# One 512-column matmul for the z projection, its halves added at eviction, and modulation sums moved to the first out-projection

## The chip, the core and the metric

One NeuronCore of a Trainium2 chip runs the whole program. The metric is the device time of one execution in microseconds (us), lower is better. Engines are named as in the profile: PE (TensorE, matmuls; PEld its weight loads), DVE (VectorE), ACT (ScalarE), POOL (GpSimd), SP (SyncE, whose queue issues nearly all DMAs).

## The reference

Two layers on x of shape (1, 256, 2048), all float32. A conditioning vector gives each layer shift, scale and gate by a product with `ada_w`. Layer 0 is chunked gated linear attention, layer 1 an S5 state-space mixer. What the change touches is layer 0:

```python
mod = einsum('bd,lde->lbe', silu(c), ada_w) + ada_b
u = x * (1 + scale) + shift
proj = u @ w_in                                   # 2048 x 10256
q, k, v, z, g_lr = split(proj, ...)               # z: 4096 columns
...
o = o * rsqrt(mean(square(o)) + eps)              # per head of 1024 channels
y = (o * norm_g) * silu(z)
h = y @ w_out                                     # 4096 x 2048, the first out-projection
x = layer_norm(alpha * x + (1 + gate) * h, ...)
```

## The kernel before, in words

Every large product is made of three: each float32 operand is split into a high part (ACT casts it to fp32r, line 145) and the rest (DVE subtracts, line 146), and high x high, high x low and low x high are summed in PSUM. A weight tile is 256 rows by 512 columns (512 KB); a step loads one (`wload`, line 136), splits it into `hi` and `lo` (rings of three buffers each), and multiplies. `st_step` (lines 171 to 182) keeps the weights stationary and streams u's 256 tokens: for each of 4 column blocks and 2 row blocks three matmuls of 256 columns, high weights by u high (L180), high weights by u low (L181), low weights by u high (L182). `st_wide` (lines 184 to 193) is used so far by the GLU product (`gl`) alone: u's two parts lie side by side (`Pairs`), so that the high weights meet both in one matmul of 512 columns (L192) and the low weights meet u high in one of 256 (L193); the two halves of the bank are added when it is read (L1323, L1324).

The stages of layer 0: q, k and v in four blocks of rows; then z in 8 groups of 512 columns with 8 steps each (lines 884 to 900); then the first out-projection, `op` (`out_proj`, line 902), 4 column groups of 16 steps. Step (g, kp) below is step kp of group g of z, or of column group g of op. Beside the z steps, the heads of the attention are finished piece by piece (`head`, line 842): in an even group one piece a step, two PE products `pso` and three evictions (`og`, `sq` or `sqt`); then once a head the root of a mean (`psrms`, ACT's Sqrt into `sd`, L865), DVE's reciprocal (L868) and two multiplications of `og` (L872), and after the odd group `og` by silu(z) (`head_fin`, L880). At the end of each z group ACT reads the four banks with Silu (L896) into time-permuted order. There are five banks in that PSUM pool. `pump(rate)` spreads background steps over the main steps: mostly the modulation's sums (`ada_dve`, line 290), where one step loads 512 KB of `ada_w` and makes two DVE multiply-adds (L309, `acc`), and every ninth finishes a block of 512 columns. `Z_RATE` and `OP_RATE` (line 663) are background steps per main step; what is left in `bg` passes from stage to stage. A scheduler may then exchange neighbouring instructions of an engine; each engine runs its list in order.

Of the kernel before, what the change touches and what calls it, by code (L numbers as in the profile page):

```python
# [8 lines left out]
F32 = mybir.dt.float32  # L9
F32R = mybir.dt.float32r  # L10
# [23 lines left out]
def trunk(ctx, tc, x, c, ln_g, ln_b, ada_w, ada_b, gla_w_in, gla_gate_w2, gla_gate_b, gla_norm_g,  # L34
# [39 lines left out]
    def s8t(name, shape, dt=F32):  # L74
        return s8.tile([P] + shape, dt, tag="s8", name=name)
# [265 lines left out]

    u0 = Parts([s8t(f"u0h{i}", [8, T], F32R) for i in range(2)], [s8t(f"u0l{i}", [8, T], F32R) for i in range(2)])

# [316 lines left out]
    for part in range(2):  # L660
        for j in range(4):
            bg.extend(ada_dve(1, part, j))
    V_RATE, Z_RATE, OP_RATE = 0.825, 0.944, 0.755
    KEEP = (4, 6)
# [172 lines left out]


    zt_ = [s8t(f"z{h}", [8, T]) for h in range(4)]
    og, sq = [None] * 4, [None] * 4  # L840

    def head(h):
        def o_step(vt_):
# [6 lines left out]
            PE.matmul(ps[:, 128:256], lhsT=vtok[:, 1, f * P:(f + 1) * P], rhs=sts[:, h, 256:384], start=False, stop=True)  # L850
            S.activation(og[h][:, vt_, :], ps[:, :T], AF.Identity, scale=gnT[:, f:f + 1])
            if vt_ == 0:
# [8 lines left out]
        def rms():  # L861
            ps = psx(f"psrms{h}")
            PE.matmul(ps[:, :T], lhsT=ones, rhs=sq[h], start=True, stop=True)
            sd[0] = tp.tile([P, T], F32, tag="sd", name=f"sd{h}", bufs=1)
            S.activation(sd[0], ps[:, :T], AF.Sqrt, scale=1.0 / 1024.0, bias=rmseps)  # L865

# [9 lines left out]
    def head_fin(h):  # L876
        def step(i):
            sl = slice(4 * i, 4 * i + 4)
            zv = zt_[h][:, sl].rearrange("p f (s c) -> p f s c", s=8)
            V.tensor_tensor(zv, og[h][:, sl].rearrange("p f (c s) -> p f s c", s=8), zv, op=ALU.mult)  # L880
        return [lambda i=i: step(i) for i in range(2)]

    hq = []
    for g in range(8):
# [3 lines left out]
        for kp in range(8):  # L888
            for _ in range(-(-len(hq) // (8 * (2 - g % 2) - kp))):
                hq.pop(0)()  # L890
            w = split(wload(win, 2 * kp, 6144 + g * 512, f"z{g}{kp}"), f"z{g}{kp}")
            st_step(banks, u0, w, kp, 15)
            pump(Z_RATE)
        for f in range(4):
            i = (g * 4 + f) % 8
            S.activation(zt_[g // 2][:, i, :].rearrange("p (s c) -> p c s", s=8), banks[f][:, :T].rearrange("p (c s) -> p c s", s=8), AF.Silu)  # L896
        if g % 2 == 1:
# [536 lines left out]
```

## Time and profile before

| | |
|---|---|
| time, median of 3 runs | 1849.08 us (1848.76 to 1849.77) |
| the profiled execution's own time | 1845.55 us |
| its span, first to last instruction | 1843.8 us |
| PE / DVE / ACT busy | 97% / 77% / 49% |
| granted TensorE clock, mean | 0.994 |
| z stage (first to last z matmul) | 372.5 to 586.1 us |
| first out-projection | 586.1 to 765.5 us |
| HBM traffic over the span | 243 GB/s |

A time in the profile is counted from the span's start. Busy time of PE counts each matmul from its start to its modelled end, and neighbours overlap, so the distance from start to start is what a matmul takes of PE's time. On DVE and ACT a row's duration overlaps the next one by some hundredths of a microsecond. What an engine waited for stands with the idle time before an instruction.

### The profile page before, as it was taken

What the parts mean: (1) busy time and instruction counts of PE and PEld (TensorE: products, weight loads), DVE (VectorE), ACT (ScalarE), POOL (GpSimd) and SP (SyncE); (2) the same over time, 40 slices, a digit from 0 to 9 for tenths busy, and PEclk for the clock granted to TensorE, in tenths of its full rate; (3) what the DMA queues carried; (4) which work ended last, traced back from release to release, by engine and by line L of the source; (5) the groups of instructions that cost most, each with busy time, mean ns of one, the idle gap of its engine ahead of it and who ended that gap; (6) DMA issues with size and microseconds to landing.
All of it is one profiled execution on the core that took longest, in us unless ns stands there. A gap on an engine that the chain in (4) does not pass through costs nothing.

```text
span 1843.8 us, 33865 instructions
## 1 busy us (share of the span) xinstructions
PE 1793.7 (97%) x13619; PEld 1587.9 (86%) x13619; DVE 1426.4 (77%) x1890; ACT 898.7 (49%) x1252; POOL 68.1 (4%) x76
## 2 busy tenths in 40 slices
PE   6999999999999999999999999999999999999997
PEld 4777798799999888799999999989888888888885
DVE  4667875989999988697899789889677775557556
ACT  3533465655556333654544544545544544444332
POOL 0000000000000000002123210000000000000000
PEclk9999999999999999999999999999999999999999
DMA  9887976789889998575655477999688886668653
GB/s 354 321 319 251 326 230 213 219 296 325 285 277 325 336 353 287 172 221 158 178 156 150 138 211 213 240 246 249 223 275 268 274 277 208 190 192 326 193 184 92
DMA packets 244182, 449.48 MB, mean 244 GB/s; under 512 B 19540, under 2 KB 49678, under 8 KB 242742
## 3 DMA queue, kind: packets, MB, share of 16 engines
q1 hardware_dynamic: 240088, 437.86, 74.1%
q0 software_dynamic: 3168, 8.41, 1.6%
q8 instruction: 107, 1.75, 0.4%
q10 hardware_dynamic: 768, 1.05, 0.2%
q14 instruction: 51, 0.42, 0.1%
HBM read 432.81 MB, written 14.42 MB: 243 GB/s over the span
## 4 chain that ended last, share of the span: by engine, by line
PE 85%; DVE 8%; DMA 2%; ACT 2%; issue 2%; SPq 0%; DVEq 0%; ACTq 0%
PE gl L192 13%; PE gl L193 6%; PE op L168 6%; PE op L167 6%; PE op L169 6%; PE z L182 3%; PE z L180 3%; PE z L181 3%; PE sz L180 3%; PE v L168 3%; PE sz L181 3%; PE sz L182 3%; PE v L169 3%; PE v L167 3%; PE su L180 2%; PE su L182 2%
## 5 line engine op out<-in xcount | busy, mean ns | idle before, releaser
L146 DVE TENSOR_TENSOR logl<-wgl,higl 128x1024 fp32r<-128x1024 f32 x128 | 156.5, 1224 | 113.2 <-ACT higl L145 109.7
L145 ACT CAST higl<-wgl 128x1024 fp32r<-128x1024 f32 x128 | 134.5, 1052 | 170.0 <-PE gl L192 160.9
L192 PE MATMUL gl<-yp,higl 128*128 128x512 f32 x512 | 178.4, 393 | 0.1
L192 PE MATMUL gl<-yb,higl 128*128 128x512 f32 x512 | 178.3, 393 | 0.0
L145 ACT CAST hio<-wo 128x1024 fp32r<-128x1024 f32 x96 | 101.3, 1055 | 155.7 <-PE op L169 142.8
L146 DVE TENSOR_TENSOR loo<-wo,hio 128x1024 fp32r<-128x1024 f32 x96 | 117.3, 1223 | 65.0 <-ACT hio L145 63.0
L309 DVE SCALAR_TENSOR_TENSOR acc<-wa,cs,acc 128x512 f32<-128x512 f32 x215 | 160.5, 747 | 2.7
L180 PE MATMUL su<-u1h,hisu 128*128 128x256 f32 x512 | 153.4, 301 | 1.8 <-DVE vv L1082 1.8
L180 PE MATMUL sz<-u1h,hisz 128*128 128x256 f32 x512 | 149.7, 292 | 1.2 <-ACT zs L1264 1.2
L180 PE MATMUL z<-u0h,hiz 128*128 128x256 f32 x512 | 148.7, 290 | 0.0
L182 PE MATMUL su<-u1h,losu 128*128 128x256 f32 x512 | 145.6, 285 | 0.4 <-DVE losu L146 0.4
L182 PE MATMUL z<-u0h,loz 128*128 128x256 f32 x512 | 145.0, 283 | 0.9 <-DVE loz L146 0.9
L181 PE MATMUL su<-u1l,hisu 128*128 128x256 f32 x512 | 145.8, 285 | 0.0
L182 PE MATMUL sz<-u1h,losz 128*128 128x256 f32 x512 | 144.8, 283 | 0.2 <-DVE losz L146 0.2
L181 PE MATMUL sz<-u1l,hisz 128*128 128x256 f32 x512 | 144.7, 283 | 0.0
L181 PE MATMUL z<-u0l,hiz 128*128 128x256 f32 x512 | 144.7, 283 | 0.0
L193 PE MATMUL gl<-yb,logl 128*128 128x256 f32 x512 | 142.8, 279 | 0.0
L193 PE MATMUL gl<-yp,logl 128*128 128x256 f32 x512 | 141.6, 279 | 0.0
L145 ACT CAST hisz<-wsz 128x1024 fp32r<-128x1024 f32 x64 | 66.9, 1050 | 103.7 <-PE sz L181 58.3
L192 PEld LDWEIGHTS gl<-yp,higl 128*128 128x128 f32 x512 | 95.8, 187 | 22.1 <-issue 0.8
L192 PEld LDWEIGHTS gl<-yb,higl 128*128 128x128 f32 x512 | 95.9, 187 | 21.9
L145 ACT CAST hisu<-wsu 128x1024 fp32r<-128x1024 f32 x64 | 66.7, 1050 | 94.8 <-PE su L181 70.0
(321 smaller groups left out, 5022.5 us busy)
## 6 DMA issues: line engine op xcount, KB each, us to landing
wgl<-in_s_w_glu SPq DMA_DIRECT2D x128, 512.0 KB, 4.7
wa<-in_ada_w SPq DMA_DIRECT2D x115, 512.0 KB, 5.1
wv<-in_gla_w_in SPq DMA_DIRECT2D x64, 512.0 KB, 6.5
wz<-in_gla_w_in SPq DMA_DIRECT2D x64, 512.0 KB, 5.1
wsu<-in_s_w_in SPq DMA_DIRECT2D x64, 512.0 KB, 3.7
wsz<-in_s_w_in SPq DMA_DIRECT2D x64, 512.0 KB, 4.7
wo<-in_s_w_out SPq DMA_DIRECT2D x64, 512.0 KB, 4.6
a<-in_ada_w SPq DMA_DIRECT2D x31, 1024.0 KB, 9.7
```

The lines of the kernel that those rows point to most:

```text
L145: S.copy(hi, w)
L146: last_lo[0] = V.tensor_tensor(lo, w, hi.bitcast(F32), op=ALU.subtract).ins
L167: PE.matmul(banks[tt], lhsT=uh, rhs=hi[:, kk, :], start=(k == first), stop=False)
L168: PE.matmul(banks[tt], lhsT=uh, rhs=lo[:, kk, :], start=False, stop=False)
L169: last_mm[0] = PE.matmul(banks[tt], lhsT=ul, rhs=hi[:, kk, :], start=False, stop=(k == last)).ins
L180: PE.matmul(o, lhsT=wh, rhs=u.hi(k), start=(k == first), stop=False)
L181: PE.matmul(o, lhsT=wh, rhs=u.lo(k), start=False, stop=False)
L182: last_mm[0] = PE.matmul(o, lhsT=wl, rhs=u.hi(k), start=False, stop=(k == last)).ins
L192: PE.matmul(banks[f], lhsT=hi[:, kk, fs], rhs=u.both(k), start=(k == 0), stop=False)
L193: PE.matmul(banks[f][:, :T], lhsT=lo[:, kk, fs], rhs=u.hi(k), start=False, stop=(k == last))
L309: V.scalar_tensor_tensor(acc[0], w[:, kk, :], cs[:, k:k + 1], acc[0], op0=ALU.mult, op1=ALU.add)
```

## The change

u is kept as `Pairs` (4 tiles with both parts), z uses `st_wide`, and at the end of a group ACT copies the right half of a bank to SBUF, DVE adds the left half to it, and ACT applies Silu from SBUF. The time permutation of `og` and `sd` moves from `head_fin`'s read to the writes of ACT, so that `head_fin` multiplies in plain order. `Z_RATE` goes from 0.944 to 0.84, `OP_RATE` from 0.755 to 0.9.

```diff
--- before.py
+++ after.py
@@ -339,7 +339,7 @@
         for tt in range(2):
             dma(xr[tt][:, c0:c1], x[0, tt * P:(tt + 1) * P, c0:c1])
 
-    u0 = Parts([s8t(f"u0h{i}", [8, T], F32R) for i in range(2)], [s8t(f"u0l{i}", [8, T], F32R) for i in range(2)])
+    u0 = Pairs([s8t(f"u0p{i}", [4, 2, T], F32R) for i in range(4)])
 
     def hilo(hi, lo, src):
         S.copy(hi, src)
@@ -660,7 +660,7 @@
     for part in range(2):
         for j in range(4):
             bg.extend(ada_dve(1, part, j))
-    V_RATE, Z_RATE, OP_RATE = 0.825, 0.944, 0.755
+    V_RATE, Z_RATE, OP_RATE = 0.825, 0.84, 0.9
     KEEP = (4, 6)
     GATE_AT = 15
     SCAN_RATE = 1.728
@@ -836,6 +836,13 @@
     y0 = Parts([], [])
 
 
+    def steps_first(ap):
+        return ap.rearrange("p (s c) -> p c s", s=8)
+
+    def by_chunk(ap):
+        return ap.rearrange("p (c s) -> p c s", s=8)
+
+
     zt_ = [s8t(f"z{h}", [8, T]) for h in range(4)]
     og, sq = [None] * 4, [None] * 4
 
@@ -848,7 +855,7 @@
             ps = psx(f"pso{f}")
             PE.matmul(ps[:, 0:256], lhsT=vtok[:, 0, f * P:(f + 1) * P], rhs=sts[:, h, 0:256], start=True, stop=False)
             PE.matmul(ps[:, 128:256], lhsT=vtok[:, 1, f * P:(f + 1) * P], rhs=sts[:, h, 256:384], start=False, stop=True)
-            S.activation(og[h][:, vt_, :], ps[:, :T], AF.Identity, scale=gnT[:, f:f + 1])
+            S.activation(steps_first(og[h][:, vt_, :]), by_chunk(ps[:, :T]), AF.Identity, scale=gnT[:, f:f + 1])
             if vt_ == 0:
                 S.activation(sq[h], ps[:, :T], AF.Square)
             else:
@@ -862,7 +869,7 @@
             ps = psx(f"psrms{h}")
             PE.matmul(ps[:, :T], lhsT=ones, rhs=sq[h], start=True, stop=True)
             sd[0] = tp.tile([P, T], F32, tag="sd", name=f"sd{h}", bufs=1)
-            S.activation(sd[0], ps[:, :T], AF.Sqrt, scale=1.0 / 1024.0, bias=rmseps)
+            S.activation(steps_first(sd[0]), by_chunk(ps[:, :T]), AF.Sqrt, scale=1.0 / 1024.0, bias=rmseps)
 
         def inv():
             V.reciprocal(sd[0], sd[0])
@@ -876,8 +883,7 @@
     def head_fin(h):
         def step(i):
             sl = slice(4 * i, 4 * i + 4)
-            zv = zt_[h][:, sl].rearrange("p f (s c) -> p f s c", s=8)
-            V.tensor_tensor(zv, og[h][:, sl].rearrange("p f (c s) -> p f s c", s=8), zv, op=ALU.mult)
+            V.tensor_tensor(zt_[h][:, sl], og[h][:, sl], zt_[h][:, sl], op=ALU.mult)
         return [lambda i=i: step(i) for i in range(2)]
 
     hq = []
@@ -889,11 +895,14 @@
             for _ in range(-(-len(hq) // (8 * (2 - g % 2) - kp))):
                 hq.pop(0)()
             w = split(wload(win, 2 * kp, 6144 + g * 512, f"z{g}{kp}"), f"z{g}{kp}")
-            st_step(banks, u0, w, kp, 15)
+            st_wide(banks, u0, w, kp, 15)
             pump(Z_RATE)
         for f in range(4):
             i = (g * 4 + f) % 8
-            S.activation(zt_[g // 2][:, i, :].rearrange("p (s c) -> p c s", s=8), banks[f][:, :T].rearrange("p (c s) -> p c s", s=8), AF.Silu)
+            zl = tp.tile([P, T], F32, tag="uf", name=f"zl{g}{f}", bufs=2)
+            S.copy(zl, banks[f][:, T:])
+            V.tensor_tensor(zl, banks[f][:, :T], zl, op=ALU.add)
+            S.activation(steps_first(zt_[g // 2][:, i, :]), by_chunk(zl), AF.Silu)
         if g % 2 == 1:
             hq += head_fin(g // 2)
             if g == 1:
```

How the instructions move, at three places. The number at a name's end is the buffer's. First, ACT at the end of z group 0 (`z_3449` to `z_3452` are its four banks, `hiz_3834` the cast of step (1, 1), `hiz_3869` that of (1, 2)), before:

```order
L145 CAST hiz_3834<-wz_3832 128x1024
L851 ACTIVATE og_3453<-pso_3744,vt 128x256
L856 ACTIVATE sqt_3748<-pso_3744 128x256
L896 ACT_TABLE_LOAD
L896 ACTIVATE z_3445<-z_3449 128x32x8
L896 ACTIVATE z_3445<-z_3450 128x32x8
L896 ACTIVATE z_3445<-z_3451 128x32x8
L896 ACTIVATE z_3445<-z_3452 128x32x8
L145 CAST hiz_3869<-wz_3867 128x1024
L865 ACT_TABLE_LOAD
L865 ACTIVATE sd_3795<-psrms_3793,kst 128x256
L145 CAST hiz_3904<-wz_3902 128x1024
```

and of the change, from the second of the four copies on (`hiz_3797` is step (1, 2)):

```order
L903 COPY zl_3721<-z_3450 128x256
L905 ACT_TABLE_LOAD
L905 ACTIVATE z_3445<-zl_3717 128x32x8
L905 ACTIVATE z_3445<-zl_3721 128x32x8
L903 COPY zl_3725<-z_3451 128x256
L903 COPY zl_3729<-z_3452 128x256
L872 ACT_TABLE_LOAD
L872 ACTIVATE sd_3739<-psrms_3737,kst 128x32x8
L905 ACT_TABLE_LOAD
L905 ACTIVATE z_3445<-zl_3725 128x32x8
L905 ACTIVATE z_3445<-zl_3729 128x32x8
L145 CAST hiz_3797<-wz_3795 128x1024
```

The cast of step (1, 2) stood behind one table load and ahead of the Sqrt; now it stands behind three table loads, the copies and the Sqrt. Ahead of the first copy stand, in this order, the cast of (1, 1), a `gate` eviction (L329), `og` and `sqt`. At the other six turns between z groups no Sqrt falls among the Silus.

Second, DVE at the same place, before (`loz_3870` belongs to step (1, 2), `loz_3905` to (1, 3)):

```order
L146 TENSOR_TENSOR loz_3870<-wz_3867,hiz_3869 128x1024
L309 SCALAR_TENSOR_TENSOR acc_3741<-wa_3897,cs,acc_3741 128x512
L868 RECIPROCAL sd_3795<-sd_3795 128x256
L309 SCALAR_TENSOR_TENSOR acc_3741<-wa_3897,cs,acc_3741 128x512
L872 TENSOR_TENSOR og_3453<-og_3453,sd_3795 128x1024 x2
L146 TENSOR_TENSOR loz_3905<-wz_3902,hiz_3904 128x1024
```

and of the change (`loz_3798` belongs to (1, 2)):

```order
L904 TENSOR_TENSOR zl_3717<-z_3449,zl_3717 128x256
L904 TENSOR_TENSOR zl_3721<-z_3450,zl_3721 128x256
L309 SCALAR_TENSOR_TENSOR acc_3714<-wa_3790,cs,acc_3714 128x512
L904 TENSOR_TENSOR zl_3725<-z_3451,zl_3725 128x256
L904 TENSOR_TENSOR zl_3729<-z_3452,zl_3729 128x256
L875 RECIPROCAL sd_3739<-sd_3739 128x256
L879 TENSOR_TENSOR og_3453<-og_3453,sd_3739 128x1024 x2
L146 TENSOR_TENSOR loz_3798<-wz_3795,hiz_3797 128x1024
L146 TENSOR_TENSOR loz_3821<-wz_3818,hiz_3820 128x1024
```

The subtraction of step (1, 2) came ahead of the reciprocal; it now comes behind the reciprocal and both multiplications.

Third, DVE in op's first column group, around its tenth to thirteenth step, before:

```order
L146 TENSOR_TENSOR loo_6205<-wo_6202,hio_6204 128x1024
L309 SCALAR_TENSOR_TENSOR acc_5960<-wa_6198,cs,acc_5960 128x512
L346 TENSOR_TENSOR ly_6164<-z_3448,hy_6163 128x512
L146 TENSOR_TENSOR loo_6231<-wo_6228,hio_6230 128x1024
L346 TENSOR_TENSOR ly_6164<-z_3448,hy_6163 128x512
L305 TENSOR_SCALAR acc_6250<-wa_6248,cs 128x512
L146 TENSOR_TENSOR loo_6256<-wo_6253,hio_6255 128x1024
```

and of the change:

```order
L146 TENSOR_TENSOR loo_5769<-wo_5766,hio_5768 128x1024
L309 SCALAR_TENSOR_TENSOR acc_5715<-wa_5762,cs,acc_5715 128x512
L346 TENSOR_TENSOR ly_5724<-z_3448,hy_5723 128x512
L309 SCALAR_TENSOR_TENSOR acc_5715<-wa_5786,cs,acc_5715 128x512
L146 TENSOR_TENSOR loo_5793<-wo_5790,hio_5792 128x1024
L309 SCALAR_TENSOR_TENSOR acc_5715<-wa_5786,cs,acc_5715 128x512
L346 TENSOR_TENSOR ly_5724<-z_3448,hy_5723 128x512
L309 SCALAR_TENSOR_TENSOR acc_5715<-wa_5810,cs,acc_5715 128x512
L146 TENSOR_TENSOR loo_5817<-wo_5814,hio_5816 128x1024
```

Two sums stand between subtractions where one stood. From step (0, 2) to step (0, 13) of op the list of DVE holds 19 multiply-adds where it held 13; both hold one product of `head_fin`.

## Rows read from the trace of the kernel before

**Rows 1.** The page: busy time of the engines (share of the span, instructions), and the chain of work that ended last, by engine.

```profile
PE 1793.7 (97%) x13619; PEld 1587.9 (86%) x13619; DVE 1426.4 (77%) x1890; ACT 898.7 (49%) x1252; POOL 68.1 (4%) x76
...
PE 85%; DVE 8%; DMA 2%; ACT 2%; issue 2%; SPq 0%; DVEq 0%; ACTq 0%
```

**Rows 2.** Windows of time: the z stage, op's first column group, and a stretch of its second. Columns: window, its length, busy time (instructions) of PE, PEld, DVE, ACT, POOL, granted clock, DMA share, GB/s.

```profile
372.50:586.10 213.60, 212.69 (x1703) 208.44 (x1702) 191.43 (x230) 127.02 (x194) 0.00 (x0) 1.00 0.89 304
...
586.10:630.00 43.90, 43.90 (x199) 36.12 (x198) 40.29 (x51) 19.77 (x23) 0.00 (x0) 1.00 0.98 300
630.00:675.00 45.00, 44.90 (x202) 36.88 (x201) 39.55 (x48) 16.87 (x16) 0.00 (x0) 1.00 1.05 386
```

**Rows 3.** Timeline of PE inside a z step (start, duration, then engine, line, operation, out<-in; all rows of the timelines below are read so).

```profile
449.93 0.28 PE L182 MATMUL z<-u0h,loz 128*128 128x256 f32 x1
...
450.29 0.28 PE L182 MATMUL z<-u0h,loz 128*128 128x256 f32 x1
...
451.73 0.28 PE L182 MATMUL z<-u0h,loz 128*128 128x256 f32 x1
```

**Rows 4.** Timeline of PE inside `gl` steps; between the first and the last row lie 15 pairs of L192 and L193.

```profile
1399.78 0.39 PE L192 MATMUL gl<-yp,higl 128*128 128x512 f32 x1
1400.01 0.28 PE L193 MATMUL gl<-yp,logl 128*128 128x256 f32 x1
...
1404.98 0.39 PE L192 MATMUL gl<-yp,higl 128*128 128x512 f32 x1
```

**Rows 5.** Groups by line and shape, whole span: count | busy us, mean ns of one | idle us before them and what ended it.

```profile
L309 DVE SCALAR_TENSOR_TENSOR acc<-wa,cs,acc 128x512 f32<-128x512 f32 x215 | 160.5, 747 | 2.7
...
L168 PE MATMUL v<-lov,u0h 128*128 128x512 f32 x256 | 103.8, 406 | 7.8 <-DVE lov L146 7.8
...
L146 DVE TENSOR_TENSOR loz<-wz,hiz 128x1024 fp32r<-128x1024 f32 x64 | 77.9, 1217 | 19.7 <-ACT hiz L145 19.7
...
L896 ACT ACTIVATE z<-z 128x256 f32<-128x256 f32 x32 | 18.3, 682 | 0.2
...
L880 DVE TENSOR_TENSOR z<-og,z 128x1024 f32<-128x1024 f32 x8 | 17.1, 2136 | 0.2 <-ACT z L896 0.2
...
L1324 DVE TENSOR_TENSOR sg<-gl,sg 128x256 f32<-128x256 f32 x32 | 12.6, 415 | 0.5 <-ACT sg L1323 0.5
...
L1224 ACT COPY xS<-psxs 128x256 f32<-128x256 f32 x32 | 11.5, 360 | 1.4 <-PE psxs L1222 1.4
...
L872 DVE TENSOR_TENSOR og<-og,sd 128x1024 f32<-128x1024 f32 x8 | 9.5, 1217 | 0.0
```

**Rows 6.** Timeline of ACT at the turn from z group 0 to group 1 (in brackets the idle time before it and what ended it), and a later `gate` eviction.

```profile
397.58 1.05 ACT L145 CAST hiz<-wz 128x1024 fp32r<-128x1024 f32 x1 [2.00 <-PE z L181]
398.53 0.47 ACT L851 ACTIVATE og<-pso,vt 128x256 f32<-128x256 f32 x1
...
399.30 1.28 ACT L896 ACT_TABLE_LOAD   x1
400.59 2.07 ACT L896 ACTIVATE z<-z 128x256 f32<-128x256 f32 x4
402.44 1.07 ACT L145 CAST hiz<-wz 128x1024 fp32r<-128x1024 f32 x1
403.53 1.28 ACT L865 ACT_TABLE_LOAD   x1
404.82 0.48 ACT L865 ACTIVATE sd<-psrms,kst 128x256 f32<-128x256 f32 x1
...
427.81 0.68 ACT L329 ACTIVATE gate<-psg,ones 128x512 f32<-128x512 f32 x1
```

**Rows 7.** Timeline of DVE at the same turn.

```profile
405.35 1.75 DVE L868 RECIPROCAL sd<-sd 128x256 f32<-128x256 f32 x1
...
407.58 2.36 DVE L872 TENSOR_TENSOR og<-og,sd 128x1024 f32<-128x1024 f32 x2
409.85 1.22 DVE L146 TENSOR_TENSOR loz<-wz,hiz 128x1024 fp32r<-128x1024 f32 x1
```

**Rows 8.** Timeline of PE at the same turn: the last matmul of group 0, the first of steps (1, 0) and (1, 2), and in step (1, 3) the second matmul and the third, the first to use its `loz`.

```profile
400.91 0.28 PE L182 MATMUL z<-u0h,loz 128*128 128x256 f32 x1
...
401.27 0.47 PE L180 MATMUL z<-u0h,hiz 128*128 128x256 f32 x1
...
407.21 0.28 PE L180 MATMUL z<-u0h,hiz 128*128 128x256 f32 x1
...
410.21 0.28 PE L181 MATMUL z<-u0l,hiz 128*128 128x256 f32 x1
411.13 0.38 PE L182 MATMUL z<-u0h,loz 128*128 128x256 f32 x1 [0.64 <-DVE loz L146]
```

**Rows 9.** op's first column group: DVE's subtractions of steps (0, 2) and (0, 13), PE's first matmuls of the same steps (three timelines), and the largest wait of ACT in op with its total, times and longest.

```profile
589.14 1.22 DVE L146 TENSOR_TENSOR loo<-big,hio 128x1024 fp32r<-128x1024 f32 x1
...
618.18 1.22 DVE L146 TENSOR_TENSOR loo<-wo,hio 128x1024 fp32r<-128x1024 f32 x1
...
591.61 0.39 PE L167 MATMUL op<-hio,hy 128*128 128x512 f32 x1
...
622.70 0.39 PE L167 MATMUL op<-hio,hy 128*128 128x512 f32 x1
...
ACT hio L145 <- PE op L169: 86.6, 51, 2.6
```

## The prediction

> **What bounds the kernel now.** I read the page first: PE is busy 97% of the span and makes up 85% of the chain that ended last, DVE 8% [rows 1]. Then windows by stage [rows 2]. In the z stage PE is busy 212.69 of 213.60 us, DVE 191.43 and ACT 127.02, at full clock (1.00, the 2.4 GHz level) and a DMA share of 0.89. So PE sets the pace, ACT has 86 us to spare, DVE little more than 20 us. In the first out-projection (op) PE is again the bound, with DVE at 40.29 of 43.90 us in the first column group; DMA there runs at a share of 1.05 and 386 GB/s, and yet ACT's casts wait for PE to release buffers, 86.6 us in 51 times [rows 9]. A microsecond taken from z's matmuls is therefore a microsecond of the span, as long as ACT and DVE still deliver `hi` and `lo` in time. That the turns between groups are the weak place is seen in rows 6 to 8: after the first turn the third matmul of step (1, 3) came 0.92 us after the second, though 0.12 is its due [rows 3, 8].
>
> **The matmuls.** The change removes 1536 matmuls of 256 columns and adds 512 of 512 and 512 of 256. Five triples take 451.73 - 449.93 = 1.80 us, 0.360 each [rows 3]. The same wide and narrow pair runs in `gl`: 15 pairs in 1404.98 - 1399.78 = 5.20 us, 0.3467 each [rows 4]. The saving is 0.0133 x 512 = **6.8 us**, all of it on the path. A z step of 8 triples goes from 2.88 to 2.77 us.
> The row of `gl` says that two starts cost less than three at equal columns. Against that stands the Trainium skill, "TensorE: Matmul & The Clock Gate", section "Back-to-back issue gap": its table gives 262 cycles for 256 columns and 518 for 512. By it a triple costs 786 cycles and a pair 780, so the edit would be worth 6 cycles a pair, an estimated 1.3 us in all, and the sum below an estimated +2.3 in place of -3.2. Rows 3 and 4, taken from this kernel's own float32r operands, show five times that saving, and the sum goes by them.
>
> **The eviction.** Each of 32 banks was read by one Silu of 0.68 us (L896). Now ACT copies 256 columns (nearest row: 0.36, L1224), DVE adds (nearest row: 0.415, L1324), and ACT applies Silu from SBUF; I keep 0.68 for it, since the permuted order is the same [rows 5]. ACT gains 32 x 0.36 = 11.5 us, and the permuted write of `og` and `sd` adds between nothing and 0.32 us each (0.68 against the plain 0.36), at most 11 us over 36. Cover: ACT's 86 idle us. Without it this would be 11.5 to 23 us. DVE gains 32 x 0.415 = 13.3 us. It loses 0.92 us at each product of `head_fin`, which becomes a plain one (2.136 against L872's 1.217), six of eight in z: 5.5 us; and the moved sums: 0.104 x 64 = 6.7 background steps fewer, six of them sums, 12 x 0.75 = 9.0 us [rows 5]. DVE's total in z is 1.2 us lower, its window 6.8 shorter: about as tight as now. What matters is order, at the turns.
>
> **The first turn, walked.** Let G be the start of the last matmul of group 0 (400.91). Now [rows 6 to 8]: cast (1, 1) at G-3.3, one table load, four Silus in 2.07, cast (1, 2) at G+1.5, Sqrt, reciprocal, two multiplications, and `loz` of (1, 3) only from G+8.9 to G+10.2; PE paid 0.8 us for that. In the new order ACT first casts (1, 1), which waits for PE's step (0, 6) and so begins at G-3.2, ends at G-2.15; `gate` 0.65 to G-1.5; `og` and `sqt` 0.77 (398.53 to 399.30) to G-0.7; two copies to G; a table load of 1.28 to G+1.3; two Silus, half of 2.07 and a little, to G+2.4; two copies to G+3.1; a table load to G+4.4; Sqrt 0.48 to G+4.9; a table load to G+6.2; two Silus to G+7.3; then cast (1, 2), 1.07, to G+8.3. DVE takes the reciprocal from G+4.9, the multiplications from G+6.6, `loz` (1, 2) from G+8.9 (4.5 us from reciprocal to `loz`, less the 0.5 of a sum that stood between [rows 7]) to G+10.1. PE reached (1, 2) 6.3 us after G (407.21) and would reach it at G+6.1 with two shorter steps; its second matmul needs `lo` at G+6.3. It waits until G+10.1: 3.8 us, against the 0.8 of now, **+3.0 us**. Ends: 0, if ACT gets through its pieces 3 us earlier than walked and PE pays the 0.8 of now, and 4.5, if the permuted writes take the whole 0.32 each. Behind this wait DVE has buffers to fill ahead, and the casts of the following steps need no wait: it is not repeated in group 1.
>
> **The other six turns.** No Sqrt and at most one table load falls among the Silus there. The third add, which frees the bank of the next group's fourth column block, comes about 2.4 us after G (copy behind a load and two Silus as above, then 0.415) and sometimes behind a `loz`; the block is due 0.36 + 3 x 0.69 = 2.4 us after G [rows 4, 8], or 0.6 later where a `pso` comes first. I take 0.05 each, **+0.3**, between 0 and 2 us each (one `loz` and one sum in front, 1.2 + 0.75).
>
> **The first out-projection.** 0.145 x 64 = 9.3 background steps more. DMA: 16 steps bring two more loads of 512 KB, 2.7 us of it at 386 GB/s; cover is the buffers' lead (the casts wait for PE, not for DMA), without it 2.7 us a column group. DVE: `loo` of (0, 2) ends at 590.36, 1.25 us before PE starts that step, and that of (0, 13) at 619.40, 3.3 us before [rows 9]: DVE gains 2.05 us on the way. Six sums more cost up to 6 x 0.75 = 4.5, the plain product returns 0.9: 3.6 us, which leaves it 0.3 us late if it starts level. It does: the last turn's adds hold `loo` (0, 2) back to about G+4.6, due at G+5.9. I take **+0.3**, ends 0 and 3.6. Afterwards nothing is late next: the second column group needs four subtractions, sums and evictions DVE could do at 39.55 of 45 us [rows 2], and the list of sums runs out some steps sooner than now.
>
> **Elsewhere.** u's new tiles change the scheduler's order a little in the q, k, v blocks: third weight load of the first block behind two loads of `ada_w`, some sums behind subtractions in the second; the same instructions, level again at each block's end. PE waited 7.8 us in all for `lo` there [rows 5]; I take 0, ends -1.3 and +1.3, two sums of 0.75 less overlap. POOL issues nothing new; SP's queue carries the same bytes.
>
> **Sum.** -6.8 + 3.0 + 0.3 + 0.3 = **-3.2 us**. The profiled execution took 1845.55, outside the three runs' 1848.76 to 1849.77; its own would become 1842.3. The median of the runs, 1849.08, becomes **1845.9**, 0.17% less. 0.2% (3.7 us, to 1845.4) is what a measurement of this kernel can tell from no change, so the forecast lies within it, next to its edge.
>
> **Rivals.**
> - *The turn costs no more than now.* ACT's chain is shorter than walked, and PE keeps nearly all: -6.8 + 0.6, **1842.9**. For it: PE now rides over 10 us of the same pieces with 0.8 lost. Against it: the three table loads stand in the list. 0.27, faster.
> - *DVE in op takes it back.* Its 3.6 us are paid by PE in full: -6.8 + 3.0 + 0.3 + 3.6, **1849.2**. For it: 40.29 of 43.90. Against it: the 2.05 us that it gains there. 0.13, no change.
> - *Every turn holds PE.* In the six others an add stands behind a `loz` and a sum: 6 x 2 more, **1857.6**, slower. It decides once the third add ends later than 2.4 us (3.0 with a `pso`) after a group's last matmul. For it: DVE at 90% in z, and in-order lists in which ACT waits for DVE and DVE for ACT. Against it: the order has the adds early. 0.08.
> - *Columns alone count.* Pair and triple stream the same 768 columns; if the pair took the triple's 0.360 in z, nothing would be saved and the 3.6 stay: **1852.7**, just within 0.2%. Rows 4 speak against it. 0.03. The rule behind it is that of the Trainium skill's page above, whose figures would make it an estimated 1.3 us less.
>
> **How the numbers follow.** The forecast's own case has 0.49; its ends (first turn 0 to 4.5, op 0 to 3.6, opening -1.3 to 1.3) spread it, and I give a third of it, 0.15, to a gain over 3.7 us, 0.02 to a loss over it. Faster 0.27 + 0.15 = 0.42; within 0.2% 0.32 + 0.13 + 0.03 = 0.48; slower 0.08 + 0.02 = 0.10. The range goes from the first rival with the opening's and the turn's gain (1842.9 - 1.3 - 0.6) to a little beyond the second and the forecast's upper ends: 1841.0 to 1851.3.
>
> **What would show it.** Right: z pairs at 0.347 from start to start; one wait of 3 to 4 us at step (1, 2), by `hiz` and then `loz`; z 3 to 4 us shorter; op as long as now within 0.5 us. Wrong: no such wait at the first turn (first rival), idle PE in op under L146 (second), waits of 1 us or more at several turns, put down to DVE's add or to ACT (third), a pair at 0.358 (fourth), or a difference that lies before 372 or after 772 us.

## The result, and the profile after

The changed kernel takes **1853.88 us** (median of 20 runs) beside 1849.36 of the kernel before (20 runs of the same session): 1.0024 times as long, interval [1.0015, 1.0033], so 4.5 us slower. Forecast were 1845.9 and no more than 1851.3. The profiled execution of the change has a span of 1853.8 us (1855.58 in all).

The page of the change, busy time and chain, against [rows 1]:

```profile
PE 1794.4 (97%) x13107; PEld 1560.4 (84%) x13107; DVE 1428.1 (77%) x1922; ACT 916.7 (49%) x1286; POOL 68.3 (4%) x76
...
PE 83%; DVE 8%; DMA 5%; issue 2%; ACT 2%; SPq 0%; DVEq 0%; ACTq 0%
```

512 matmuls fewer, and PE is as busy as before; DMA's part of the chain went from 2% to 5%. Where it went is seen in windows: z and the four column groups of the first out-projection (op), columns as in [rows 2].

```profile
372.20:582.40 210.20, 207.87 (x1183) 179.79 (x1182) 187.92 (x247) 141.58 (x221) 0.00 (x0) 1.00 0.86 292
582.40:632.90 50.50, 47.51 (x202) 37.69 (x201) 44.57 (x58) 21.77 (x27) 0.00 (x0) 0.97 1.00 295
632.90:678.30 45.40, 45.40 (x209) 37.83 (x208) 38.45 (x50) 16.88 (x16) 0.00 (x0) 1.00 1.05 386
678.30:725.60 47.30, 46.32 (x209) 37.57 (x209) 40.17 (x51) 16.86 (x16) 0.00 (x0) 1.00 0.92 329
725.60:770.60 45.00, 45.00 (x201) 36.64 (x201) 34.78 (x45) 19.45 (x20) 0.00 (x0) 1.00 0.56 187
```

z begins at 372.2 (372.5 before) and is 3.4 us shorter, nearly the 3.5 that the sum had for it. Op is 8.9 us longer: first column group 50.5 us and third 47.3, where the kernel before takes 44.7 and 45.4.

**z's first turn.** ACT and DVE after group 0, whose last matmul starts at G = 399.79; compare [rows 6, 7]:

```profile
401.35 0.69 ACT L903 COPY zl<-z 128x256 f32<-128x256 f32 x2
402.05 1.28 ACT L872 ACT_TABLE_LOAD   x1
403.35 0.74 ACT L872 ACTIVATE sd<-psrms,kst 128x256 f32<-128x256 f32 x1
404.10 1.28 ACT L905 ACT_TABLE_LOAD   x1
405.40 1.14 ACT L905 ACTIVATE z<-zl 128x256 f32<-128x256 f32 x2
406.32 2.96 ACT L145 CAST hiz<-wz 128x1024 fp32r<-128x1024 f32 x3
```

```profile
404.12 1.75 DVE L875 RECIPROCAL sd<-sd 128x256 f32<-128x256 f32 x1 [1.56 <-ACT sd L872]
405.91 2.36 DVE L879 TENSOR_TENSOR og<-og,sd 128x1024 f32<-128x1024 f32 x2
408.18 2.35 DVE L146 TENSOR_TENSOR loz<-wz,hiz 128x1024 fp32r<-128x1024 f32 x2
```

and PE there, steps (1, 1) and (1, 2), against [rows 8]:

```profile
403.11 0.39 PE L192 MATMUL z<-u0p,hiz 128*128 128x512 f32 x1
403.34 0.27 PE L193 MATMUL z<-u0p,loz 128*128 128x256 f32 x1
403.45 0.40 PE L192 MATMUL z<-u0p,hiz 128*128 128x512 f32 x1
...
405.53 0.40 PE L192 MATMUL z<-u0p,hiz 128*128 128x512 f32 x1
405.77 0.28 PE L193 MATMUL z<-u0p,loz 128*128 128x256 f32 x1
407.44 1.19 PE L192 MATMUL z<-u0p,hiz 128*128 128x512 f32 x4 [1.39 <-ACT hiz L145]
409.46 0.38 PE L193 MATMUL z<-u0p,loz 128*128 128x256 f32 x1 [0.82 <-DVE loz L146]
```

The wait stands where it was walked: cast (1, 2) ends at G+7.6 (walked +8.3), `loz` at G+9.6 (+10.1). PE runs the four wide matmuls that need `hi` alone first, so it loses 1.39 + 0.82 = 2.2 us and not 3.8.

**op's first column group.** ACT's waits from 610 to 630 (total, times, longest), and the windows around PE's long wait:

```profile
ACT hio L145 <- DMA big<-in_gla_w_out: 6.1, 2, 5.9
```

```profile
615.00:622.60 7.60, 7.27 (x31) 5.31 (x30) 5.24 (x7) 1.05 (x1) 0.00 (x0) 1.00 1.01 249
622.60:624.90 2.30, 0.18 (x1) 0.00 (x1) 1.37 (x3) 1.04 (x1) 0.00 (x0) 1.00 1.05 384
624.90:629.60 4.70, 4.18 (x11) 3.01 (x12) 4.55 (x5) 2.10 (x2) 0.00 (x0) 0.66 1.04 384
```

The cast of a step waits 5.9 us for a weight load, and PE stands. ACT's casts at the same place in the kernel before show how near this was already:

```profile
622.90 1.06 ACT L145 CAST hio<-big 128x1024 fp32r<-128x1024 f32 x1 [1.66 <-PE op L169]
625.77 1.05 ACT L145 CAST hio<-big 128x1024 fp32r<-128x1024 f32 x1 [1.81 <-DMA big<-in_gla_w_out]
```

One cast is released by a weight load and not by PE, 0.15 us behind the 2.72 us pace of its neighbours. PE lost nothing by it, but the lead was used up there before a load was added. What DMA did: the 40 slices of 599 to 626 us in the change (busy tenths, GB/s, total),

```profile
DMA  9894799989997999999999699979999999999999
GB/s 343 322 270 155 273 343 194 170 149 203 212 231 146 200 212 234 194 209 316 428 209 167 106 182 200 279 143 200 212 231 197 194 322 388 388 388 379 391 373 379
DMA packets 2833, 6.84 MB, mean 253 GB/s; under 512 B 271, under 2 KB 271, under 8 KB 2575
```

and in the kernel before, same 27 us:

```profile
DMA  9799999999997999999999899999999999999999
GB/s 252 237 376 391 385 300 358 310 215 219 243 218 155 237 155 291 325 249 206 203 255 206 185 228 182 255 322 388 385 382 388 388 388 388 379 379 388 388 388 388
```

DMA is busy throughout in both, yet behind SP's eight loads of x (599.5 to 609.8 issued) it moves about 200 GB/s, and 388 once they are in. Before, the buffers' lead carried PE over that stretch; with the sums' added loads ahead of it, it no longer does.

**op's third column group.** DVE at its start, in the change (`ot` is the product that reads the finished group's bank):

```profile
673.75 1.53 DVE L309 SCALAR_TENSOR_TENSOR acc<-wa,cs,acc 128x512 f32<-128x512 f32 x2
677.40 0.69 DVE L923 TENSOR_TENSOR ot<-op,gate 128x512 f32<-128x512 f32 x1 [2.12 <-PE op L169]
678.01 1.22 DVE L146 TENSOR_TENSOR loo<-wo,hio 128x1024 fp32r<-128x1024 f32 x1
...
681.67 1.21 DVE L146 TENSOR_TENSOR loo<-big,hio 128x1024 fp32r<-128x1024 f32 x1
```

DVE is not short of time here: it stands idle 2.12 us, since `ot` comes ahead of two `loo` in its list and waits for PE's last matmul of the group. PE's weight loads then wait for these `loo` (PEld L168 <- L146: 2.2 us in 3 times from 676 to 725.6; over all of op 5.5 in 9, against 1.0 in 3 before), and PE itself stands 0.9 us. In the kernel before `ot` stands one `loo` later in the list.

### The profile page after: what moved, and what is told of

The parts are those of the page before. It is cut to its first block, busy times and chain, and to the rows that moved or that the text cites. A ratio compares the mean times of both kernels' runs of the same rounds, so it can differ in the third digit from the quotient of the medians.

```text
span 1853.8 us, 32916 instructions
## 1 busy us (share of the span) xinstructions
PE 1794.4 (97%) x13107; PEld 1560.4 (84%) x13107; DVE 1428.1 (77%) x1922; ACT 916.7 (49%) x1286; POOL 68.3 (4%) x76
## 3 DMA queue, kind: packets, MB, share of 16 engines
q10 hardware_dynamic: 768, 1.05, 0.2%
## 4 chain that ended last, share of the span: by engine, by line
PE 83%; DVE 8%; DMA 5%; issue 2%; ACT 2%; SPq 0%; DVEq 0%; ACTq 0%
PE gl L192 13%; PE gl L193 7%; PE op L168 6%; PE z L192 6%; PE op L169 6%; PE op L167 6%; PE z L193 3%; PE v L168 3%; PE sz L180 3%; PE v L169 3%; PE v L167 3%; PE sz L182 3%; PE sz L181 3%; PE su L180 2%; PE su L182 2%; PE su L181 2%
## 5 line engine op out<-in xcount | busy, mean ns | idle before, releaser
L146 DVE TENSOR_TENSOR logl<-wgl,higl 128x1024 fp32r<-128x1024 f32 x128 | 156.3, 1223 | 114.0 <-ACT higl L145 110.5
L192 PE MATMUL z<-u0p,hiz 128*128 128x512 f32 x512 | 184.7, 404 | 1.4 <-ACT hiz L145 1.4
L192 PE MATMUL gl<-yp,higl 128*128 128x512 f32 x512 | 178.9, 394 | 0.1
L192 PE MATMUL gl<-yb,higl 128*128 128x512 f32 x512 | 178.7, 394 | 0.0
L146 DVE TENSOR_TENSOR loo<-wo,hio 128x1024 fp32r<-128x1024 f32 x97 | 118.4, 1221 | 62.0 <-ACT hio L145 61.9
L193 PE MATMUL gl<-yb,logl 128*128 128x256 f32 x512 | 143.1, 279 | 0.0
L193 PE MATMUL z<-u0p,loz 128*128 128x256 f32 x512 | 142.1, 280 | 0.8 <-DVE loz L146 0.8
L193 PE MATMUL gl<-yp,logl 128*128 128x256 f32 x512 | 142.0, 280 | 0.0
L192 PEld LDWEIGHTS z<-u0p,hiz 128*128 128x128 f32 x512 | 96.0, 188 | 22.6 <-ACT hiz L145 1.7
L192 PEld LDWEIGHTS gl<-yp,higl 128*128 128x128 f32 x512 | 95.8, 187 | 22.3 <-issue 0.5
L192 PEld LDWEIGHTS gl<-yb,higl 128*128 128x128 f32 x512 | 95.9, 187 | 22.1
```

What stands on the lines that cost most here:

```text
L146: last_lo[0] = V.tensor_tensor(lo, w, hi.bitcast(F32), op=ALU.subtract).ins
L192: PE.matmul(banks[f], lhsT=hi[:, kk, fs], rhs=u.both(k), start=(k == 0), stop=False)
L193: PE.matmul(banks[f][:, :T], lhsT=lo[:, kk, fs], rhs=u.hi(k), start=False, stop=(k == last))
```

## The experiments

Stage lengths come from each kernel's profile (z and op from the first to the last start of their matmuls, column groups from start to start), ratios from timed runs against the kernel before. The code of the opening and of the later stage `sz` is the same everywhere in the table but for the order of the opening's instructions; its `sz` nevertheless took 255.6 to 263.2 us from profile to profile. So stages say where, ratios how much. Two differences between rows of the table are the granted clock and not the kernel: in op_spread, evict_later and x_turns it falls to 0.50 for a while behind the first turn's wait, so that z's group 1 takes 26.7 to 26.8 us in place of the change's 25.2 to 25.4, with the same list of z instructions; and in the change, sums_only, sqrt_later and half_sums it falls so in op's first group (some 1.5 us).

| kernel | z | op | column groups 0 to 3 | of before |
|---|---|---|---|---|
| before, before_again | 213.5, 213.5 | 179.3, 179.3 | 44.7 44.9 45.4 44.2 | 1 |
| the change | 210.1 | 188.2 | 50.5 45.4 47.3 44.9 | 1.0024 [1.0015, 1.0033] |
| after_again | 210.3 | 185.3 | 47.3 45.8 47.3 44.9 | one run |
| wide_only | 211.8 | 179.2 | 44.6 44.9 45.4 44.2 | 0.9995 [0.9981, 1.0008] |
| sums_only | 211.7 | 190.0 | 52.3 45.4 47.3 44.9 | 1.0022 [1.0012, 1.0031] |
| op_spread | 211.3 | 184.5 | 44.5 46.8 47.8 45.4 | 1.0013 [1.0004, 1.0021] |
| sqrt_later | 210.0 | 188.9 | 51.3 45.4 47.3 44.9 | 1.0014 [0.9999, 1.0029] |
| x_zeros | 210.0 | 180.1 | 45.0 45.4 45.4 44.2 | 0.9996 [0.9984, 1.0008] |
| half_sums | 209.8 | 187.6 | 50.6 45.4 47.3 44.2 | 1.0022 [1.0010, 1.0034] |
| x_halves | 210.2 | 184.3 | 45.5 46.5 47.4 44.9 | 1.0014 [0.9999, 1.0029] |
| evict_later | 211.5 | 182.9 | 47.1 45.4 45.4 44.9 | 1.0019 [1.0003, 1.0034] |
| halves_evict | 210.6 | 182.7 | 45.5 46.9 45.4 44.9 | 0.9998 [0.9988, 1.0009] |
| no_add | 206.1 | 183.9 | 46.2 45.4 47.4 44.9 | one run |
| x_rows | 210.4 | 180.7 | 45.0 45.4 45.4 44.9 | 0.9993 [0.9982, 1.0005] |
| wide_sqrt | 209.9 | 179.2 | 44.6 44.9 45.4 44.2 | **0.9984 [0.9972, 0.9997]** |
| all_fix | 209.8 | 187.2 | 50.7 46.2 45.4 44.9 | 1.0007 [0.9995, 1.0019] |
| x_turns | 211.5 | 184.3 | 46.7 45.4 47.3 44.9 | 1.0014 [1.0005, 1.0023] |
| x_two_queues | 211.4 | 187.8 | 50.1 45.5 47.3 44.9 | 1.0032 [1.0018, 1.0046] |
| all_two_queues | 209.2 | 186.1 | 49.9 45.8 45.4 44.9 | 1.0009 [0.9998, 1.0019] |

**Which half of the change.** wide_only, and sums_only (the kernel before with the new rates):

```
-    V_RATE, Z_RATE, OP_RATE = 0.825, 0.84, 0.9      # wide_only; sums_only the reverse
+    V_RATE, Z_RATE, OP_RATE = 0.825, 0.944, 0.755
```

> The change with the sums put back where they were (rates 0.944 in z and 0.755 in the first out-projection): the wide matmuls, the eviction by copy, add and Silu and the new order of og and sd alone. Theory A (the out-projection pays for the sums it took over: 188.2 us in place of 179.3 in the two profiles, while z gave the 3.4 us that were forecast): z about 210 to 211 us, out-projection 179 to 181, the whole 1846 to 847 us, 3 to 4 us under the kernel before. Theory B (the out-projection loses by how z hands over to it, its last eviction and the products behind it, or by lateness in stages the change does not touch): about 1852 to 1855, as the change.

> The kernel before with the rates of the change alone (0.84 in z, 0.9 in the out-projection), matmuls of 256 columns and Silu from the bank as they were. Theory A: z unchanged to 1 us less, out-projection 5 to 9 us longer, the whole 1854 to 1857. Theory B: within 1.5 us of the kernel before, 1848 to 1851.

Op's loss belongs to the moved sums: 179.2 without them, 190.0 with them alone. The wide form by itself gives z 1.7 us, half of what A expected, since the sums' leaving gives the other 1.8. Both of sums_only's stages went beyond A's bounds (up to 1 us less in z, 5 to 9 more in op), and its whole, 1851.95, stayed under the 1854 to 1857; wide_only's whole gained 0.9 us by its ratio and not 3 to 4, and its interval takes in no change. Part of sums_only's 52.3 is VectorE: PE stands 1.84 us for a `loo` at 597.7, behind a product of `head_fin` that still takes 2.15 us there. In the change, where that product is a plain one, this wait is gone.

**How op's sums are spread.**

```
-                pump(npump)
+                pump(npump if l else (0.6 if cg == 0 else 1.0))
```

> The change with the out-projection's sums spread otherwise: rate 0.6 in its first column group, where x is loaded as well, and 1.0 in the three others, so that all four together take the same 57.6 steps. Theory A1 (within A, the wait for data in the first column group is the larger part: two casts there came 4 to 5 us late behind SP's loads of x): first column group back to about 44 us from 48, the whole 1849 to 1851, unless the other groups lose more at 1.0. Theory A2 (DVE is what is short, wherever the sums stand): the waits for lo in column groups 2 and 3 grow from 3 us to 5 to 8, the whole 1853 to 1857. Theory B: 1853 to 1855.

A1 for the first group (44.5), and the three others pay 5.5 us more than before: both effects stand side by side.

**The first turn.**

```
+  for _ in range(0 if (g, kp) == (1, 0) else -(-len(hq) // (8 * (2 - g % 2) - kp))):
```

> The change with head 0's steps held back by one step at (1, 0): its Sqrt comes after the cast of (1, 2) and one step later, and that cast before the last two Silus of group 0. If the first turn's chain costs what the trace of the change shows there (about 2 to 3 us over the turn before the change), z becomes 207 to 208 us and the whole 1851 to 1852; if the wait only moves to the next step, z stays at 210 and the whole at 1854.

A miss: the stall in group 1 (start to start beyond what a pair takes) falls from 2.7 to 1.4 us and the group from 25.2 to 24.3, but group 2 grows from 26.7 to 27.6, and z goes only from 210.1 to 210.0. Op's first group repeats the change's loss (51.3).

**Data or VectorE in op.** x_zeros, half_sums and x_halves:

```
-  hooks[0, 12 + t] = [lambda t=t: [dma(res0[t][32 * s:32 * s + 32], xv[4 * t + s]) for s in range(4)]]
+  hooks[0, 12 + t] = [lambda t=t: nc.gpsimd.memset(res0[t], 0.0)]                  # x_zeros
-            for kk in range(2):
+            for kk in range(1 if halve else 2):                                    # half_sums
+  for cg, k, sl in ((0, 12, slice(0, 1024)), (1, 8, slice(1024, 2048))):           # x_halves
+      hooks[cg, k + t] = [lambda t=t, sl=sl: [dma(res0[t][32 * s:32 * s + 32, sl], xv[4 * t + s, :, sl]) ...
```

> The change with x left out of the first out-projection: GpSimd writes zeros where the eight loads of x (2.1 MB) went; all sums, weight loads and matmuls stay. In the three kernels with 0.9 the first column group took 50.5 to 52.3 us against 44.6 with 0.755. Theory D (data: in that group the loads of x on top of 16 weight loads and some 14 loads for the sums are more than the DMA brings in 44 us): first column group 44.5 to 45.5, columns groups 1 to 3 as in the change (45.4, 47.3, 44.9), the whole 5 to 6 us under the change in its profile, 1848 to 1850. Theory V (VectorE is short there: eight products and sums in the same steps): first group still 49 to 52, the whole 1852 to 1855.

> The change with one of the two multiply-adds of every background step left out from the first out-projection on; its loads all stay, so DMA carries the same and VectorE some 43 us less. Theory D: first column group still 49 to 51, groups 1 to 3 back to 44.9, 45.4 and 44.2 as with rate 0.755 (their 3.1 us are lateness of VectorE): the whole 3 us under the change, 1850 to 1851. Theory V: first group 44.6 and the others back too: 8 to 9 us less in op, 1844 to 1847.

> The change with x loaded in two halves of 1024 columns: the first at (0, 12) and (0, 13), the second at (1, 8) and (1, 9), which takes 1.05 MB out of the first column group, about what the higher rate puts in. Theory D: first group 45 to 47, second 45.4 to 46.5, the whole 4 to 5 us under the change's profile, 1849 to 1850. Theory V: first group 49 to 52.

Theory D holds for the first group: 45.0 without x, 50.6 with half of DVE's sums, 45.5 with half of x elsewhere (which then costs the second group 1.1). Of its other three it is right for the fourth (44.2 with half of the sums) and misses in the second by 0.5 and in the third: half of the sums gone and still 47.3. That group is short neither of data nor of DVE; without x the instructions stand in another order, and it takes 45.4.

**Two executions of one kernel.** The change and the kernel before, unedited:

> The change itself once more, for a second profile: does the out-projection take its 188 us again (50.5, 45.4, 47.3, 44.9 by column group), and do the 3.8 us by which the later stage sz was longer (257.6 to 261.4, code unchanged) come again? If these belong to the execution and not to the change, sz lies at 257 to 259 and the span at 1849 to 1852.

> The kernel before once more, for a second profile: which stages differ between two executions of one kernel. By the two profiles of the change (span 1853.8 and 1842.7): z within 0.3 us, column group 0 of the out-projection and the stages v and sz by 2 to 6 us. Here column group 0 should repeat its 44.7 within 0.5, since its loads were in time.

Op's loss came again, smaller: first group 47.3, the others within 0.4. `sz` took 255.6 us in place of 261.4, and the kernel before 260.5 in place of 257.6: so those 3.8 us belonged to the execution, though the second profile's `sz` and its span (1842.7) lie below what was expected (257 to 259, 1849 to 1852). Z and op of the kernel before repeat to 0.1.

**Order at the column groups' turns.**

```
-                if pend:
+                if pend and kp:
...
             def gated(tt):
+                with tc.issue_after(last_lo[0]):
...
```

> The change with the product that reads a column group's bank (ot) held behind the lo of step 2 of the next group, in place of step 0 or 1. Why: with one multiply-add of each step left out, column group 2 took the same 47.3 us, so VectorE's work is not what is short there; in the trace of the change VectorE stands idle 2.1 us in front of ot, which waits for the group's last matmul, and lo of (2, 0) and (2, 1) stand behind it; in the kernel before, and in the one without x, ot comes later and the group takes 45.4. Theory O (order): group 2 back to 45.4, group 3 from 44.9 to 44.2 to 44.6, group 0 still 47 to 52, whole 2 to 2.5 us under the change. Theory V (VectorE is short after all): 47 and more again, only later in the group.

> The change with both: x loaded in halves, in column groups 0 and 1, and ot behind the lo of step 2. If the out-projection's 6 to 9 us are data in group 0 and order in groups 1 to 3, it comes back to 180 to 181.5 us, z stays at 210.2, and the whole is 1.5 to 3 us under the kernel before. If either was only a symptom of too much work on VectorE: op 183 or more and the whole not under the kernel before.

Theory O: third group 45.4. It holds over the whole table: where 32 `loo` of op stand ahead of the third group's first `ot`, that group takes 47.3 to 47.8 us, and where 33 or 34 do (before, wide_only, wide_sqrt, x_zeros, x_rows and the kernels with this edit), 45.4. The fourth group missed (44.9, expected 44.2 to 44.6), and the whole, by ratio, gained 0.9 us on the change in place of 2 to 2.5, less than the two intervals can tell apart. DVE at the same place, `ot` now behind two `loo`, and no wait:

```profile
675.78 1.22 DVE L146 TENSOR_TENSOR loo<-wo,hio 128x1024 fp32r<-128x1024 f32 x1
676.91 1.53 DVE L309 SCALAR_TENSOR_TENSOR acc<-wa,cs,acc 128x512 f32<-128x512 f32 x2
678.36 1.22 DVE L146 TENSOR_TENSOR loo<-big,hio 128x1024 fp32r<-128x1024 f32 x1
679.50 0.74 DVE L309 SCALAR_TENSOR_TENSOR acc<-big,cs,acc 128x512 f32<-128x512 f32 x1
680.16 0.69 DVE L927 TENSOR_TENSOR ot<-op,gate 128x512 f32<-128x512 f32 x1
```

Both edits together leave 182.7, 1.2 us more than expected, and a whole that can't be told from the kernel before: with x's second half the second group takes 46.9, 1.5 more than in the change.

**z's matmuls without the eviction.** `S.activation(..., by_chunk(banks[f][:, :T]), AF.Silu)`, without the copy and the add:

> The change without the second half of each bank: Silu reads the first half alone, as in the kernel before, so no copy and no add (the product of w's hi with u's lo is left out of z). It parts z's matmuls from the eviction. If the pair is worth 6.8 us and the eviction costs the first turn 3.0 and the others 0.3, z comes to 206.7 to 207.2 us from 210.2; if the pair is worth 5.1 (0.350 in z by the trace of the change) and the eviction costs 1.6 to 2.5, z is 207.7 to 208.6; if the first turn's wait comes from the new order of og and sd or the table loads and not from the copies and adds, z stays at 209.5 or more.

206.1: less than any of the three cases had; by one profile, the eviction costs more than they said. Against sums_only, with the same sums and the old matmuls, the wide form gives 211.7 - 206.1 = 5.6 us; copies and adds cost 210.2 - 206.1 = 4.1, of it 2.7 - 0.2 = 2.5 at the first turn. Where the clock did not fall, kernels with one list of z instructions differ by up to 0.7 us, so these parts are good to some tenths.

**Bytes or form of x's loads.**

```
+  hooks[0, 12 + t] = [lambda t=t: [dma(res0[t][:, 512 * s:512 * s + 512], x[0, t * P:(t + 1) * P, 512 * s:512 * s + 512]) for s in range(4)]]
```

> The change with x loaded in rows as they lie in memory: eight loads of 128 partitions by 512 columns in place of eight of 32 partitions by 2048, the same 2.1 MB at the same places; the rows of x come in another order than the computation wants, nothing else is left out. In the trace of the change DMA is busy the whole time around x's loads and yet moves some 200 to 230 GB/s there, against 379 to 391 behind them. Theory F (it is the form of x's loads that takes the time): column group 0 comes to 44.5 to 45.5 us, and the rate stays near 300 to 390 GB/s through the loads. Theory B (it is the bytes): group 0 stays at 47 to 52.

It is the form: the same 2.1 MB in loads of 128 partitions, first group 45.0. The form is three things at once, the number of partitions, the length of a row (8 KB or 2 KB) and the order of reading; no run parts them. DMA over 602 to 629 us of that kernel:

```profile
DMA  9799988977999999999999999999999999999999
GB/s 297 249 370 370 346 258 246 255 243 203 270 367 388 404 404 407 401 385 388 388 385 391 382 388 385 391 382 388 388 388 388 388 376 388 382 407 364 379 379 385
DMA packets 5076, 9.69 MB, mean 359 GB/s; under 512 B 357, under 2 KB 357, under 8 KB 5074
```

The slow stretch lasts some 4 us and not 17: 359 GB/s on average against 253.

**The versions to which this points.** wide_sqrt is wide_only with the edit of sqrt_later; all_fix is the change with those of evict_later and sqrt_later, and x's loads one by one:

```
+  hooks[0, 6 + 4 * t + s] = hooks.get((0, 6 + 4 * t + s), []) + [lambda t=t, s=s: dma(res0[t][32 * s:32 * s + 32], xv[4 * t + s])]
```

> The wide matmuls with the old rates (as wide_only) and head 0's steps held back by one at (1, 0): the version to which the runs so far point for a kernel faster than both. z 210 to 211.8 us (wide_only 211.8; the change went from 210.1 to 210.0 by this edit alone), out-projection 179.2, the whole 1 to 4 us under the kernel before.

> The change with all three edits: ot behind the lo of step 2, head 0's steps held back by one at (1, 0), and x's eight loads, in the form they have, one by one at the steps (0, 6) to (0, 13) in place of four each at (0, 12) and (0, 13). Theory F: each load still moves slowly, but next to weight loads that have more time to come: group 0 45 to 46, out-projection 180 to 181.5, z 210, the whole 1 to 3 us under the kernel before. If the form costs its time wherever it stands, group 0 stays at 47 or more and the whole is at or over the kernel before.

wide_sqrt beats both kernels: 1844.85 us against 1848.67, with an interval that ends just below 1. Its z and op's first group, in windows:

```profile
374.50:584.60 210.10, 208.87 (x1192) 180.54 (x1191) 195.12 (x260) 140.48 (x220) 0.00 (x0) 1.00 0.89 305
584.60:629.20 44.60, 44.60 (x203) 36.79 (x202) 40.86 (x53) 22.57 (x27) 0.00 (x0) 1.00 1.00 317
```

all_fix misses: spread out, x's loads cost the first group the same (50.7).

**Why the form costs.** x_turns and x_two_queues; all_two_queues adds evict_later and sqrt_later to the second.

```
+  [dma(res0[t][32 * s:32 * s + 32], xv[4 * t + s]) for s in (0, 2, 1, 3)]                            # x_turns
+  [(S.dma_start if s > 1 else dma)(res0[t][32 * s:32 * s + 32], xv[4 * t + s]) for s in (0, 2, 1, 3)]  # x_two_queues
```

> The change with the four loads of x at each place in another order: partitions 0 to 31, 64 to 95, 32 to 63, 96 to 127 in place of ascending. Same bytes, same form, same places. x_rows (128 partitions) took column group 0 from 50.5 to 45.0 us, so the form costs the time. If it costs because one 32-partition load uses half of the ways into SBUF, and neighbouring loads that use the other half can run beside it, group 0 comes to 45 to 46; if the loads go through one after the other whatever their partitions, it stays at 47 to 52. The Trainium skill, "SBUF — State Buffer", section "Door 1: The DMA port swizzle", says that partitions 0 to 63 reach 8 of 16 ports and 64 to 127 the other 8.

> The change with the loads of partitions 64 to 127 of x issued by ACT's queue and those of 0 to 63 by SP's. ACT's list has them earlier than SP's (the first two before the last casts of z, the others in the first steps of the out-projection), so that half of x's slow bytes leave the stretch in which SP's loads are late, and both halves can be in flight together. Group 0 45 to 46 us and the whole 2 to 4 us under the change if x's form in SP's queue is the whole of group 0's loss; 47 or more if the same slow time is merely paid from another queue.

> The change with x from two queues, ot behind the lo of step 2 and head 0's steps held back by one: all three causes met at once. z 209.8 to 210.5 us, out-projection 180 to 181, the whole 2 to 4 us under the kernel before, about as wide_sqrt (0.9984). If group 0 stays at 47 or more, op 182.5 or more and the whole within 0.1% of the kernel before.

x_turns is not decisive: 46.7 lies between its two cases, 0.6 under the better profile of the change, and no_add, with x in ascending order, took 46.2. The second queue does not help (50.1 and 49.9). With x in this form the time is paid wherever the loads stand in this stretch; why, these runs leave open.

## Why the prediction was wrong, point by point

- **The failed step: op at +0.3 us**, ends 0 and 3.6. Its DMA half was "cover is the buffers' lead", two more loads at 386 GB/s. That figure, and the share of 1.05 that the text gives for the first column group, stand in the row of the second; the first group's own row reads 0.98 and 300 GB/s [rows 2]. DMA was busy there while moving 300. At that rate the 2.3 added loads (64 x 0.145 / 4, 1.2 MB) are 4.0 us, not 2.7, and lead is all that could hide them. There was none left: a cast already waited for its weight load at 625.77. What had used it up, x's eight slow loads, is no term of the sum; with x in rows the added loads cost this group 0.3 us (x_rows, 45.0). Measured for the group: 2.6 and 5.8 in the change's two profiles, 7.6 in sums_only. Not all of it is data: 1.6 of the 5.8 are the clock, as told below, and 1.8 of the 7.6 a wait for `loo`.
- **"The casts wait for PE, not for DMA"** was read from a sum over all four column groups (86.6 us in 51 times, [rows 9]). A sum tells what waits most, not how much is left where it is tightest.
- **"Afterwards nothing is late next"** failed by 3.1 us in groups 1 to 3 (0.5, 1.9 and 0.7). In the third group DVE had time enough, as half_sums shows; the order was not looked at: with the sums moved, `ot` stands ahead of one more `loo`. The fourth group's 0.7 goes when half of the sums do; the second's 0.5 stays open.
- **DVE in op** (the second rival): its place was right, its mechanism wrong. Its 1849.2 is still short of 1853.9.
- **z: -3.5 forecast, -3.4 measured, by errors that cancel.** Matmuls -5.6 and not -6.8: a z pair takes 0.350 (median, start to start), `gl`'s 0.347 [rows 4]. Eviction +4.1 and not +3.3. The sums' leaving -1.8, counted as nothing: 0.9 at the first turn, 0.8 of eight `psmod` matmuls that went along (0.10 each). Together -3.3; without the third term -1.5, near the 1.7 that wide_only gained in z. That the forecast for z came out near the measured -3.4 is luck.
- **The first turn** was right in mechanism and place, 2.5 for the eviction against 3.0. Without the moved sums and with the Sqrt a step later, wide_sqrt gains 3.0 us by its ratio (0.6 to 5.2); that this is near the 3.2 forecast for another kernel shows nothing for the sum.
- **The third rival** (every turn holds PE, 1857.6) is out: groups 2 to 7 stall 0.0 to 0.5 us each. So is the fourth: the pair saves its 5.6 us. By the Trainium skill, "TensorE: Matmul & The Clock Gate", section "Back-to-back issue gap", it would have been an estimated 1.3; the measurement decides, and the rows of `gl` were nearer to it.
- The median's 4.5 us is within what the two stages leave: -3.4 (-3.2 in after_again) and +6.0 to +8.9 give some +2.8 to +5.5.

## What to carry to other kernels

A DMA row's rate holds only for the loads that are in it, and a share near 1 does not tell by itself whether there is room: op's second column group, at 1.05 and 386 GB/s, takes the added loads and loses 0.5 us in all, the first, at 0.98 and 300, does not get by so. What tells is an instruction that already waits for a load, as the one cast of the kernel before does. Work that is moved to an engine with time to spare brings its loads and its place in the list along; check both in the stretch where they are tightest, not in a stage's mean. When a change has two halves, measure each alone: here the wide matmuls gave z 1.7 us, and the moved sums gave it 1.8 and took 10.7 in op.

## What the runs showed of the hardware

- Loads of 32 partitions by 8 KB rows keep DMA busy at some 200 GB/s; 128 partitions by 2 KB give 359 on average over the stretch. The Trainium skill, "SBUF — State Buffer", section "Door 1: The DMA port swizzle", says that 32 partitions reach 8 of the 16 ports, measured there at 189 GB/s against 328 for 128 partitions. The trace's rates, some 200 and 359, agree with it, though row length and order changed along with the partitions. That loads into the other half of the partitions run beside them is not seen (x_turns, mostly 200 to 280 GB/s).
- After PE's idle 2.1 us at 622.8 the granted clock of the next 4.7 us was 0.66: eight matmuls start 0.43 us apart (the 1.2 GHz level) in place of 0.23, 1.6 us of that group's loss. It is 1.00 before and in the next column group. In after_again, where the longest idle was 0.53 us, no run of matmuls is that slow. But the wait alone does not settle it: behind the same 1.4 and 0.8 us at z's first turn the clock fell to 0.50 in three kernels (op_spread, evict_later, x_turns; group 1 takes 1.3 us more) and not in the change, and behind 1.8 us in op it stayed at 1.00 in x_two_queues.
- A z step's first triple takes 0.08 us more than the others (0.437 to 0.440 against 0.360, start to start) in the 34 of 64 steps of the kernel before that stand right behind a `pso` or `psmod` matmul, and 0.18 more behind a `psrms` (4 steps); behind a z matmul it takes 0.360 in 23 of 25, and the other two contain waits. In the change it is the same (medians 0.433 behind `pso`, 0.347 behind z). So each piece of other work between two steps costs PE more than its own matmuls; why, the traces don't say.
